# Batch norm streamed through one NeuronCore: stores moved from SyncE's DMA queue to ScalarE's

## The chip, the core and the metric

The kernel runs on one NeuronCore of one Trainium2 chip. The metric is the device time of one execution in microseconds (us), lower is better. A data transfer is issued by the sequencer of an engine (SyncE, written SP in the profile, or ScalarE, written ACT) and carried out by the core's 16 DMA engines. A *ring* is the list of work that one queue has waiting at the DMA engines.

All timed runs told here were at clock 1.000.

## The reference

Batch normalisation with given statistics, in fp32: per channel a scale and a shift, nothing more.

```python
# x: (32, 256, 128, 128) float32; gamma, beta, running_mean, running_var: (256,)
def reference(x, gamma, beta, running_mean, running_var):     # cut: reshapes to (1, 256, 1, 1)
    return gamma * (x - mean) / np.sqrt(var + 1e-5) + beta
```

x has 536.9 MB and so has the result. Every byte must be loaded once and stored once.

## The kernel before

A tile is 128 channels of one image: 128 partitions x 16384 floats, 8.39 MB. There are 64 tiles and three buffers. Parameters are turned into one scale and one shift per channel at the start; then VectorE does one multiply-add per tile in place.

```python
SINGLE_QUEUE = True
NBUF = 3
...
    def issue_load(i):
        if i >= NT:
            return
        t = data.tile([P, HW], mybir.dt.float32, tag="t")
        loads[i] = nc.sync.dma_start(out=t[:], in_=xr[i])
        tiles[i] = t

    for i in range(NBUF):
        issue_load(i)
    # ... (parameters, scale_t, shift_t: cut)

    def compute(i):
        t = tiles[i]
        cb = i % NCB
        nc.vector.tensor_scalar(out=t[:], in0=t[:],
            scalar1=scale_t[:, cb : cb + 1], scalar2=shift_t[:, cb : cb + 1],
            op0=mybir.AluOpType.mult, op1=mybir.AluOpType.add)

    def store(i):
        t = tiles.pop(i)
        (nc.sync if SINGLE_QUEUE else nc.scalar).dma_start(out=outr[i], in_=t[:])

    K = NBUF - 1
    for b in range((NT + K - 1) // K):
        idxs = [i for i in range(K * b, K * b + K) if i < NT]
        for i in idxs: compute(i)
        for i in idxs: store(i)
        for i in idxs: issue_load(i + NBUF)
```

Load i+3 waits for store i, because it writes into the same buffer. All transfers leave on SyncE's queue, in the order two stores, two loads. (The framework that compiles this orders instructions itself; the compiled order was read back.)

## Time and profile before

| | before |
|---|---|
| median of the first 3 runs | 2487.14 us (2486.58 to 2490.18) |
| span of the profiled run | 2488.1 us |
| VectorE busy | 564.7 us, 23% |
| DMA busy, of 16 engines | 99.8% of the span on queue q1 |
| bytes moved, mean rate | 1073.77 MB, 432 GB/s |

The page of the kernel before, parts 1 to 3. In the rows of 40 slices each digit is the busy share in tenths (9 is 90% or more), and GB/s is what the DMA engines moved in that slice.

```profile
span 2488.1 us, 378 instructions
DVE 564.7 (23%) x69; ACT 1.6 (0%) x2; POOL 3.2 (0%) x8
...
DMA  9999999999999999999999999999999999999998
GB/s 414 429 438 433 433 429 437 436 430 431 435 436 433 428 437 436 434 428 436 433 437 428 435 435 435 426 437 436 435 427 435 436 438 426 434 437 436 432 431 378
...
q1 hardware_dynamic: 18432, 1073.75, 99.8%
```

The DMA row has no slice under 9 but the last. A nine can hide up to a tenth of idle time, so this row alone does not show that there is no hole (k1_forced, below, has forty nines and loses 8%). The share of 99.8% on q1 does, and so do the records of the single packets: from the first data packet of the kernel to the last, an engine is idle for 4.0 us in the mean. There is hardly a hole for a change of queues to fill.

The list of waits of the kernel before: engine and line, what it waited for, total us, times, longest. First the engines' own list, then that of the SyncE queue.

```profile
DVE t L86 <- DMA t<-in_x_dram: 1867.9, 63, 49.6
```

```profile
SPq L48 <- DMA out_dram<-t: 1484.0, 61, 30.2
SPq L97 <- DVE t L86: 919.2, 33, 46.4
```

SyncE spends nearly the whole span waiting, 1484 us of it in loads that need a store to finish. But a wait of the issuing sequencer costs time only if the rings run empty meanwhile. The timeline of the kernel before shows why they don't (start, duration, engine, line; "x2" is two issues merged, and the duration then reaches from the first to the last):

```profile
1014.93 19.65 SPq L48 DMA_DIRECT2D t<-in_x_dram  x2
1034.63 28.62 SPq L97 DMA_DIRECT2D out_dram<-t  x2
1054.07 8.81 DVE L86 TENSOR_SCALAR t<-t,scale_t,shift_t 128x16384 f32<-128x16384 f32 x1 [49.61 <-DMA t<-in_x_dram]
1072.99 8.81 DVE L86 TENSOR_SCALAR t<-t,scale_t,shift_t 128x16384 f32<-128x16384 f32 x1 [10.12 <-DMA t<-in_x_dram]
1092.30 19.59 SPq L48 DMA_DIRECT2D t<-in_x_dram  x2
```

Two loads go out about 19.3 us apart, each at the moment a store has landed. When the first of them is issued, the second store is still in the ring; when the second is issued, the first load is. VectorE needs 8.8 us for a tile while the second load takes 19.3. There is always a transfer behind the one that moves.

The records of the single DMA packets say the same more finely. There are 16384 data packets of 65536 bytes, 8 per engine and transfer. The median packet takes 2418 ns, for loads and stores alike, and a new group of 128 packets (one transfer) starts every 19.319 us. The records do not name the engine; where this text speaks of one engine, its packets were chained by matching each packet's start to the end of the one before.

### The profile page before, as it was taken

How to read it: one execution, taken by the hardware profiler on the slowest of the kernel's cores; microseconds unless marked ns; L12 is line 12 of the kernel's file. 1: busy time of each engine (PE TensorE's matmuls, PEld its weight loads, DVE VectorE, ACT ScalarE, POOL GpSimd, SP SyncE). 2: the span in 40 equal slices, each digit the busy share in tenths (PEclk: the TensorE clock that was granted, in tenths of full speed). 3: DMA queues.
4: the chain of work that ended last, by engine and by line, in shares of the span. 5: the costliest groups of instructions: out<-in, count | busy, mean ns of one | idle time of the engine just before them, and what ended most of it. 6: DMA issues, size and time to landing. Idle time of an engine off the chain costs nothing.

```text
span 2488.1 us, 378 instructions
## 1 busy us (share of the span) xinstructions
DVE 564.7 (23%) x69; ACT 1.6 (0%) x2; POOL 3.2 (0%) x8
## 2 busy tenths in 40 slices
DVE  2122211222112221122212222121221212212121
ACT  0000000000000000000000000000000000000000
POOL 0000000000000000000000000000000000000000
DMA  9999999999999999999999999999999999999998
GB/s 414 429 438 433 433 429 437 436 430 431 435 436 433 428 437 436 434 428 436 433 437 428 435 435 435 426 437 436 435 427 435 436 438 426 434 437 436 432 431 378
DMA packets 18562, 1073.77 MB, mean 432 GB/s; under 512 B 2176, under 2 KB 2176, under 8 KB 2176
## 3 DMA queue, kind: packets, MB, share of 16 engines
q1 hardware_dynamic: 18432, 1073.75, 99.8%
q0 software_dynamic: 128, 0.00, 0.0%
q14 instruction: 2, 0.02, 0.0%
HBM read 536.88 MB, written 536.87 MB: 432 GB/s over the span
## 4 chain that ended last, share of the span: by engine, by line
DMA 51%; another core or an unknown queue 36%; DVE 11%; SPq 0%; issue 0%; POOL 0%; DVEq 0%; POOLq 0%; PEldq 0%
DMA t<-in_x_dram 48%; DVE t L86 11%; DMA out_dram<-t 2%; DMA t<-in_running_mean_dram 1%; SPq L97 0%; POOL t L56 0%; DVEq L86 0%; POOLq L133 0%; SPq L48 0%; DVE shift_t L81 0%; DVE tmp_t L80 0%; DVEq L80 0%; PEldq L133 0%
## 5 line engine op out<-in xcount | busy, mean ns | idle before, releaser
L86 DVE TENSOR_SCALAR t<-t,scale_t,shift_t 128x16384 f32<-128x16384 f32 x64 | 564.0, 8812 | 1868.0 <-DMA t<-in_x_dram 1867.9
L78 DVE RECIPROCAL tmp_t<-tmp_t 128x2 f32<-128x2 f32 x1 | 0.2, 166 | 13.2 <-ACT tmp_t L71 13.2
L80 DVE TENSOR_TENSOR tmp_t<-t,scale_t 128x2 f32<-128x2 f32 x1 | 0.2, 160 | 7.6 <-DMA t<-in_running_mean_dram 7.6
L71 ACT ACT_TABLE_LOAD x1 | 1.3, 1283 | 12.4 <-DMA t<-in_running_var_dram 12.4
L79 DVE TENSOR_TENSOR scale_t<-t,tmp_t 128x2 f32<-128x2 f32 x1 | 0.2, 160 | 3.2 <-DMA t<-in_gamma_dram 3.2
L56 POOL DMA_DIRECT2D t<-in_running_var_dram x1 | 0.8, 839 | 0.8 <-PEq L133 0.8
L56 POOL DMA_DIRECT2D t<-in_gamma_dram x1 | 0.7, 722 | 0.0
L56 POOL DMA_DIRECT2D t<-in_beta_dram x1 | 0.7, 722 | 0.0
L56 POOL DMA_DIRECT2D t<-in_running_mean_dram x1 | 0.7, 722 | 0.0
L71 ACT ACTIVATE tmp_t<-t,eps_t 128x2 f32<-128x2 f32 x1 | 0.3, 295 | 0.0
L65 DVE MEMSET eps_t<- 128x1 f32 x1 | 0.1, 59 | 0.8 <-PEq L122 0.8
L81 DVE TENSOR_TENSOR shift_t<-t,tmp_t 128x2 f32<-128x2 f32 x1 | 0.2, 160 | 0.0
L122 POOL MEMSET const-bfloat16-1.0<- 128x1 bf16 x1 | 0.1, 96 | 0.0
L122 POOL MEMSET const-uint8-127<- 128x1 uint8 x1 | 0.1, 94 | 0.0
L122 POOL MEMSET const-float32-0.0<- 128x1 f32 x1 | 0.1, 93 | 0.2 <-issue 0.2
L122 POOL MEMSET const-float32-1.0<- 128x1 f32 x1 | 0.1, 93 | 0.0
## 6 DMA issues: line engine op xcount, KB each, us to landing
t<-in_x_dram SPq DMA_DIRECT2D x64, 38.6
out_dram<-t SPq DMA_DIRECT2D x64, 49.9
t<-in_running_var_dram POOLq DMA_DIRECT2D x1, 1.0 KB, 11.1
t<-in_gamma_dram POOLq DMA_DIRECT2D x1, 1.0 KB, 15.2
t<-in_beta_dram POOLq DMA_DIRECT2D x1, 1.0 KB, 19.5
t<-in_running_mean_dram POOLq DMA_DIRECT2D x1, 1.0 KB, 21.6
```

The costliest lines, as they stand in the source:

```text
L56: nc.gpsimd.dma_start(out=t, in_=ap_1d.rearrange("(j p) -> p j", p=P))
L65: nc.vector.memset(eps_t, eps)
L71: nc.scalar.activation(out=tmp_t[:], in_=var_t[:], func=mybir.ActivationFunctionType.Sqrt, bias=eps_t[:], scale=1.0,)
L78: nc.vector.reciprocal(out=tmp_t[:], in_=tmp_t[:])
L79: nc.vector.tensor_mul(out=scale_t[:], in0=gamma_t[:], in1=tmp_t[:])
L80: nc.vector.tensor_mul(out=tmp_t[:], in0=mean_t[:], in1=scale_t[:])
L81: nc.vector.tensor_sub(out=shift_t[:], in0=beta_t[:], in1=tmp_t[:])
L86: nc.vector.tensor_scalar(out=t[:], in0=t[:], scalar1=scale_t[:, cb : cb + 1], scalar2=shift_t[:, cb : cb + 1], op0=mybir.AluOpType.mult, ...
L122: nc = _bacc.Bacc("TRN2", target_bir_lowering=False, num_devices=1)
```

## The change

The intent: loads on SyncE's queue and stores on ScalarE's, so that both rings hold work for the DMA engines at once and a load that waits for a buffer cannot hold up a store behind it. The Trainium skill, "Perfetto Trace Analysis", section "DMA Optimizations", suggests such a split: one issuing engine for inputs and another for outputs, "Especially when there are loops or control-flow", to "allow more dynamic spread".

```diff
-SINGLE_QUEUE = True
+SINGLE_QUEUE = False
 NBUF = 3
```

## The prediction

> What bounds the kernel now: the 16 DMA engines. The utilisation slices show DMA at 9 tenths or more in all slices but the last and 414 to 438 GB/s; the mean is 432 GB/s and queue q1 took 99.8% of 16 engines' span. VectorE is busy 564 us (23%) in 64 operations of 8.8 us; the list of waits has it waiting 1868 us for loads. In the DMA packet records each of the 16384 data packets (64 KB) takes 2418 ns, load or store alike, and packets follow each other on an engine without a gap: a whole 8 MB transfer starts every 19.319 us, and this step is the same after a change of direction. An estimate from that: 128 transfers x 19.319 = 2472.8 us of engine time, against a span of 2488.1. Only about 15 us (0.6%) are not pure transfer: some 2.5 us before the first packet, a slow first transfer (21.2 us), a few steps of 19.4 to 20.0 us, and 6 to 8 us of uneven engine finish at the end.
>
> 64 KB in 2418 ns is 27.1 GB/s an engine. The Trainium skill, "DMA: Bandwidth & Descriptors", section "Where 436 GB/s comes from", puts the ceiling at 435.2 GB/s for 16 engines; the trace agrees, with 432 to 438.
>
> What the change does: it adds and removes no work. The 64 stores go from SyncE's queue to ScalarE's, which is otherwise idle (1.6 us). Issuing costs about 0.34 us per transfer, already hidden. SyncE's waits (1484 us of loads for stores, 919 us of stores for VectorE) split over two queues, but they are off the critical path: while SyncE waits, the ring still holds a transfer, so no engine starves. The change removes waits that cost nothing.
>
> What moves: instead of load, load, store, store in one ring at full speed, a load and a store share the engines, so each should take about twice 19.3 us. The skill (same page, "Issuing engines are not separate DMA queues") says such transfers interleave on the same engines and only issue time is saved. With three buffers I expect no hole: an estimate by hand with 38.6 us per shared transfer and 12 us from load landed to store issued (8.8 of VectorE, about 3 of landing and issue) leaves 8 to 15 us of slack on either ring in the steady state; when one ring is empty the other runs at full speed.
>
> On the critical path, then, only the rate of a packet counts. If alternating rings costs nothing, the time is 2480 to 2490. If each switch costs some ns (the gap at a change of transfer is 2 to 3 ns, against -4 inside one), 16384 switches over 16 engines add about 6 us. If reads and writes mixed all the time are slower than in blocks, it costs more; the trace hardly shows that mix, only about 2 us per boundary in which the engines' skew overlaps both, without a slower packet.
>
> Predicted: 2492 us, 8 in 10 within 2478 to 2525. Faster by over 2%: 0.03; within 2%: 0.82; slower by over 2%: 0.15.
>
> What would show it: two hardware queues with half of the packets each; loads and stores near 40 us or more from issue to landing; still 430 to 436 GB/s in every slice; VectorE's waits for loads still about 1870 us, evenly near 30 us each instead of 49 and 10.
>
> What would make it wrong. Faster: if an engine can overlap a load's and a store's data, the rate would pass 440 GB/s. Slower: packets longer than 2418 ns without more in flight, so GB/s below 424 in steady slices; or holes in the DMA slices, because arbitration favours one ring so much that three buffers run dry.

## The result, and the profile after

| | before | after |
|---|---|---|
| median of the first 4 runs | 2487.09 us | 2494.76 us |
| lowest, highest | 2486.58, 2490.18 | 2487.87, 2500.81 |
| span of the profiled run | 2488.1 us | 2486.1 us |
| ratio after / before | | 1.0027, 95% interval 1.0007 to 1.0047 |

A ratio is the mean time of one kernel's fast runs over that of the other's of the same rounds, so it is not quite the ratio of the medians. Note the four single times of the changed kernel: 2487.87, 2500.81, 2499.87, 2489.64. They come in two groups, and the median falls between them.

The page of the changed kernel:

```profile
span 2486.1 us, 439 instructions
DVE 564.7 (23%) x69; ACT 1.6 (0%) x2; POOL 3.2 (0%) x8
...
DMA  9999999999999999999999999999999999999999
GB/s 414 429 438 435 429 435 433 439 428 434 437 438 428 434 437 439 428 432 438 431 428 438 434 428 433 433 433 429 432 431 435 432 430 431 429 439 430 430 435 405
...
q1 hardware_dynamic: 9216, 536.88, 50.1%
q10 hardware_dynamic: 9216, 536.88, 49.8%
```

There are now two hardware queues, q1 with the loads and q10 with the stores, each with half of the packets. The rate is 428 to 439 GB/s in all slices but the first and the last, where the kernel before had 426 to 438. The waits of the changed kernel, the engines' first, then the SyncE queue's:

```profile
DVE t L86 <- DMA t<-in_x_dram: 1873.5, 63, 30.8
```

```profile
SPq L48 <- DMA out_dram<-t: 2377.4, 61, 75.0
```

VectorE waits just as long as before (1873.5 against 1867.9 us), but evenly: at most 30.8 us, where it was 49 and 10 by turns. SyncE now waits 2377 us for stores, more than before, and nothing comes of it. The timeline, cut to one period (three short stretches of it):

```profile
1005.96 0.33 SPq L48 DMA_DIRECT2D t<-in_x_dram  x1
```

```profile
1018.19 8.81 DVE L86 TENSOR_SCALAR t<-t,scale_t,shift_t 128x16384 f32<-128x16384 f32 x1 [29.74 <-DMA t<-in_x_dram]
1027.03 0.34 ACTq L97 DMA_DIRECT2D out_dram<-t  x1
```

```profile
1044.62 0.33 SPq L48 DMA_DIRECT2D t<-in_x_dram  x1
```

A load is issued at 1005.96, about 12 us before the load ahead of it has landed and released VectorE at 1018.19. A store is issued at 1027.03, 17.6 us before the store ahead of it has landed and released the next load at 1044.62. So each ring has its next transfer 12 to 17 us before it needs it. The period, 1044.62 - 1005.96 = 38.66 us for a load and a store, is twice the 19.319 us of one transfer: the same work rate in another order.

The issue-to-landing medians of the page after (part 6) rose, 38.6 to 51.1 us for a load and 49.9 to 56.1 for a store, because each transfer now gets half of the engines' time:

```profile
t<-in_x_dram SPq DMA_DIRECT2D x64, 51.1
out_dram<-t ACTq DMA_DIRECT2D x64, 56.1
```

### The profile page after: what moved, and what is told of

It is laid out like the page before. It is cut to its first block, busy times and chain, and to the rows that moved or that the text cites. A ratio compares the mean times of both kernels' runs of the same rounds, so it can differ in the third digit from the quotient of the medians.

```text
span 2486.1 us, 439 instructions
## 1 busy us (share of the span) xinstructions
DVE 564.7 (23%) x69; ACT 1.6 (0%) x2; POOL 3.2 (0%) x8
## 3 DMA queue, kind: packets, MB, share of 16 engines
q1 hardware_dynamic: 9216, 536.88, 50.1%
q10 hardware_dynamic: 9216, 536.88, 49.8%
## 4 chain that ended last, share of the span: by engine, by line
another core or an unknown queue 75%; DVE 23%; DMA 1%; issue 0%; DVEq 0%; POOL 0%; POOLq 0%; PEldq 0%
DVE t L86 23%; DMA t<-in_running_mean_dram 1%; DVEq L86 0%; POOL t L56 0%; POOLq L133 0%; DVE shift_t L81 0%; DVE tmp_t L80 0%; DVEq L80 0%; PEldq L133 0%
## 5 line engine op out<-in xcount | busy, mean ns | idle before, releaser
L86 DVE TENSOR_SCALAR t<-t,scale_t,shift_t 128x16384 f32<-128x16384 f32 x64 | 564.0, 8813 | 1873.5 <-DMA t<-in_x_dram 1873.5
## 6 DMA issues: line engine op xcount, KB each, us to landing
t<-in_x_dram SPq DMA_DIRECT2D x64, 51.1
out_dram<-t ACTq DMA_DIRECT2D x64, 56.1
t<-in_beta_dram POOLq DMA_DIRECT2D x1, 1.0 KB, 19.3
```

Source lines behind the costliest of these rows:

```text
L86: nc.vector.tensor_scalar(out=t[:], in0=t[:], scalar1=scale_t[:, cb : cb + 1], scalar2=shift_t[:, cb : cb + 1], op0=mybir.AluOpType.mult, ...
```

## The experiments

The first theory: a DMA engine has one data path of about 27.1 GB/s (65536 bytes in 2418 ns) for both directions, it was already full, and what two queues could give, the kernel before already had from its order of two stores and two loads. Rivals: loads and stores have separate ceilings that two rings could use at once; the rings' order and number don't matter at all; and, for the two groups of times, an idle stretch at the end, slower packets, or single slow engines.

### loads_only and stores_only: is there a second data path?

```diff
 # loads_only: all loads and computes, only the last tile is stored (wrong result on purpose)
-            store(i)
+            if i == NT - 1:
+                store(i)
+            else:
+                tiles.pop(i)
```

> Wrong result on purpose: all 64 loads and computes, only the last tile is stored. One data path per engine (mine): a load packet takes 2418 ns as in the full kernel, so 65 transfers x 19.32 us = 1256 us, plus about 15 of start, last compute and tail: 1262 to 1280 us. Rival, a load and a store can overlap inside an engine and each direction alone has its own ceiling: then this run would also take about 1256, but together with stores_only the sum of the two would be clearly above the time of the changed kernel (2488 to 2500). Mine: the two sums, less what each runs of the other direction, equal it within 1%.

```diff
 # stores_only: three loads and computes, then 64 stores out of those buffers (wrong on purpose)
     def issue_load(i):
-        if i >= NT:
+        if i >= NBUF:
+            tiles[i] = tiles[i % NBUF]
             return
 # ... compute(i) returns for i >= NBUF; store(i) reads tiles[i] without popping it
```

> Wrong result on purpose: 3 loads and computes, then 64 stores out of those three buffers. Mine: 67 transfers x 19.32 = 1294 us plus about 10 to 20 of start and tail: 1300 to 1315 us, packets of 2418 ns. Rival (directions have separate ceilings, or stores alone are faster than mixed): packets shorter than 2400 ns or a rate above 440 GB/s.

Measured: 1277.51 and 1303.77 us, both in the expected ranges. The busy time of the stretch from 300 to 1200 us, whose last two columns are the DMA share and the GB/s, first of loads_only, then of stores_only, then of the kernel before, then of the changed kernel:

```profile
300.00:1200.00 900.00, 410.95 (x47) 0.00 (x0) 0.00 (x0) 1.00 1.00 433
```

```profile
300.00:1200.00 900.00, 0.00 (x0) 0.00 (x0) 0.00 (x0) 1.00 1.00 433
```

```profile
300.00:1200.00 900.00, 199.31 (x23) 0.00 (x0) 0.00 (x0) 1.00 1.00 434
```

```profile
300.00:1200.00 900.00, 202.70 (x23) 0.00 (x0) 0.00 (x0) 1.00 1.00 434
```

Loads alone, stores alone and both at once on two rings all run at 433 to 434 GB/s. The sum 1277.5 + 1303.8 less the three loads and one store that were extra (4 x 19.32) is 2504.0 us, 0.6% above the changed kernel's median over 12 runs (2488.8), and each of the two runs has a start and an end of its own. There is no second path for the other direction. The first theory stands on this point. One rival is left: that the limit is not in each engine but in something that all 16 share, such as the memory. A later trace speaks against it: in after_r5 only two of the 16 engines are at work from 2465.5 to 2475 us, and each of their packets takes 2418 ns there too.

### k1_single: a test that tested nothing

```diff
-    K = NBUF - 1
+    K = 1
```

> The kernel before with batches of one instead of two: store, load, store, load on the one queue. Mine: the change was worth nothing because the batching already kept a transfer in the one ring; without it each load waits for the only transfer in the ring, so the ring runs dry once per tile, for 1.5 us (landing 0.5, issue to first packet 1.0) up to 3 us (plus the engines' uneven finish of about 1.4): 61 x 1.5 to 3 = 92 to 183 us, so 2580 to 2670 us, 4 to 7% slower. On two queues the same program is instruction for instruction the changed kernel (the streams of each engine are the same), so that is what two queues would then be worth. Rival: the ring's order doesn't matter and the engines find work anyway: within 1% of before.

Measured: 2490.52 us, ratio 1.0007 (0.9992 to 1.0021). That contradicts the expectation, and the reason is trivial: the compiled instructions of this kernel are the same as those of the kernel before, in the same order (the numbers in the buffers' names differ). The scheduler paired two stores and two loads by itself. The run is one more run of the kernel before and says nothing for or against either theory.

### k1_forced: what an unpaired order costs on one queue

```diff
-        loads[i] = nc.sync.dma_start(out=t[:], in_=xr[i])
+        with after_last():      # tc.issue_after(the DMA issued last): an issue order, no wait
+            loads[i] = nc.sync.dma_start(out=t[:], in_=xr[i])
+        last[:] = [loads[i].ins]
 # ... the same around the store
-    K = NBUF - 1
+    K = 1
```

> The run k1_single tested nothing: its compiled instructions are those of the kernel before, in the same order (the scheduler pairs two stores and two loads by itself). Here the order store, load, store, load is forced on the one queue (checked in the compiled order). Mine: each load then waits for the only transfer in the ring, the ring runs dry once per tile, for 1.5 us (landing 0.5, issue to first packet 1.0) up to 3 us (with the engines' uneven finish): 61 x 1.5 to 3, so 2580 to 2670 us, and since two queues with the same order per stream are the changed kernel, that much is what two queues are worth against an unpaired order. Rival: order doesn't matter, the engines find work anyway: within 1% of before.

Measured: 2719.15 us (2718.87 to 2719.97), ratio 1.0924 (1.0908 to 1.094). The result is correct and the direction is as expected; the size was above my range. The same stretch of this kernel, three rows of its page, and its timeline:

```profile
300.00:1200.00 900.00, 185.06 (x21) 0.00 (x0) 0.00 (x0) 1.00 0.95 394
```

```profile
DMA  9999999999999999999999999999999999999999
GB/s 417 386 401 398 389 399 388 401 387 386 400 401 401 386 386 401 386 401 401 386 399 388 401 386 401 386 400 401 387 401 386 386 401 401 400 378 394 401 396 406
...
q1 hardware_dynamic: 18432, 1073.75, 95.5%
```

```profile
999.68 8.81 DVE L95 TENSOR_SCALAR t<-t,scale_t,shift_t 128x16384 f32<-128x16384 f32 x1 [33.70 <-DMA t<-in_x_dram]
1018.99 0.33 SPq L56 DMA_DIRECT2D t<-in_x_dram  x1
1019.37 0.42 SPq L107 DMA_DIRECT2D out_dram<-t  x1
1042.33 8.81 DVE L95 TENSOR_SCALAR t<-t,scale_t,shift_t 128x16384 f32<-128x16384 f32 x1 [33.84 <-DMA t<-in_x_dram]
1061.59 0.33 SPq L56 DMA_DIRECT2D t<-in_x_dram  x1
1061.96 0.43 SPq L107 DMA_DIRECT2D out_dram<-t  x1
```

The DMA row is full of nines, and only the GB/s row and the 95.5% give the loss away. The store's tile was ready at 1008.49, when VectorE ended it, but the store stood behind a load that waited for its buffer, and went out at 1019.37. So load and store now go out together, 0.4 us apart, once in 42.6 us instead of 38.6, and between two pairs there is nothing in the ring: 394 GB/s. In the packet records there are 61 moments with no data packet in flight on any engine, 1.33 us each in the median. A restart also costs more than the empty time: the first packet of each engine after it takes 3066 ns in the mean instead of 2418 (0.65 us more), and the eighth 3677 ns (1.26 us more). These make 3.2 us; the step from restart to restart is 42.53 us, 3.89 over 2 x 19.32. The rest, about 0.65 us, is what engines lose by ending and starting at different moments (an estimate, the remainder). I had counted the empty time and the uneven end, not the longer packets after it. From the first data packet of the run to the last, an engine is idle for 121 us in the mean (4 in the kernel before) and its packets take 113 us longer in sum: the loss is half empty time, half longer packets. Why the first and the eighth packet (the last one of the load) are long was not found.

With the stores on the other queue this program compiles to the changed kernel, every engine's instructions the same but for the numbers in the buffers' names. It was compiled and compared, and not run again. So against this order the change is worth 2719 to 2489 us, over 8%. Against the pairing order it is worth nothing.

### nbuf2_single and nbuf2_split: two buffers, one queue or two

```diff
-NBUF = 3
+NBUF = 2
 # nbuf2_split also has SINGLE_QUEUE = False
```

> Two buffers, one queue; the compiled order is again two stores, two loads. Mine: the second store covers the wait of the first load and the second load covers VectorE (19.3 us of load against about 10.5 from landing to issue), so the ring never runs dry: within 0.5% of before, 2480 to 2500 us. Rival (a third buffer is what keeps the engines full): over 2540 us.

> Two buffers, two queues. Mine: now the two buffers move as they come free, and twice in two tiles both rings are empty for about 1 us or more (one buffer in VectorE, the other between its store and its load): by hand 79.1 us for two tiles instead of 77.3, and the engines' drift on top: 2520 to 2600 us, slower than the same on one queue. Rival (two rings always fill the engines better): at most the time of nbuf2_single.

Measured: 2489.08 us (ratio 1.0003, 0.9988 to 1.0018) on one queue and 2667.6 us (1.0709, 1.0686 to 1.0733) on two. The stretch of nbuf2_single, then that of nbuf2_split:

```profile
300.00:1200.00 900.00, 202.68 (x23) 0.00 (x0) 0.00 (x0) 1.00 1.00 433
```

```profile
300.00:1200.00 900.00, 193.87 (x22) 0.00 (x0) 0.00 (x0) 1.00 0.98 402
```

With two buffers the change has the opposite sign: two rings are 7% slower than one. The compiled order on one queue is still two stores, two loads, as its timeline shows:

```profile
1043.05 20.14 SPq L97 DMA_DIRECT2D out_dram<-t  x2
```

```profile
1073.33 19.65 SPq L48 DMA_DIRECT2D t<-in_x_dram  x2
```

The second store covers the wait of the first load, and the second load covers VectorE. On two queues nothing holds the transfers in pairs, and again and again one buffer is in VectorE while the other has just been stored and not yet been reloaded: at 31 moments no data packet is in flight on any engine, 0.47 us each in the median. My estimate of the empty time was about right (1.8 us for two tiles by hand; in the packets the engines' mean idle time is 62.6 us over the 32 pairs, 2.0 each), and the range was missed by a term like that in k1_forced: busy time too went up, from 2481 us per engine in the kernel before to 2605, because a tenth of the load packets took 3293 ns or more (the first packet of a load took 3269 ns in the mean). These longer packets are two thirds of the loss, and their cause stays open. The rival "two rings always fill the engines better" is out, and so is "a third buffer is what keeps the engines full".

### after_r5: where do the times near 2500 come from?

> The changed kernel again, five rounds, for the spread of its times (2488, 2490, 2500, 2501 so far, where before has 2487 to 2490). If its spread comes from the engines' state in a run, both values come again, within one chip; if it was the one chip's, they don't. Either way the ratio to before lies between 1.000 and 1.006.

Edit: none, the changed kernel again. Measured: 2500.77, 2500.47, 2483.36, 2482.87, 2482.23, 2501.16 us; ratio 1.0011 (0.9983 to 1.0039). Both groups came on one chip, while the kernel before stayed between 2485.95 and 2493.58. This time the profiled run was a late one, of 2499.0 us. The ends of two runs of the same kernel, from 2400 to 2500 us in slices of 2.5 us: first the 2486.1 us run, then the 2499.0 us run.

```profile
DMA  9999999999999999999999999999999990000000
GB/s 419 419 419 419 419 419 472 524 419 446 419 419 446 419 419 419 419 419 419 419 419 419 419 419 419 446 419 419 446 419 472 419 446 0 0 0 0 0 0 0
```

```profile
DMA  9999999999999999999999941111119999999910
GB/s 419 419 419 419 419 446 446 419 472 419 419 419 446 446 419 419 498 472 419 472 446 446 419 184 79 79 52 52 52 52 419 419 419 419 419 419 419 419 52 0
```

From about 2460 to 2475 us nearly everything is idle, about 14 us as the engines' mean, and then the last store runs alone for 20 us. The timeline of that run has VectorE on the last tile from 2466.87 to 2475.7, and the store issued at 2475.71. It looked as if this idle stretch were the cause: the last load lands late, VectorE works, nobody has anything to move.

### after_tail4: quarter the last tile

```diff
 # the changed kernel, with the last tile loaded, computed and stored in four column quarters
-        loads[i] = nc.sync.dma_start(out=t[:], in_=xr[i])
+        for a, z in parts(i):       # one part, or four for the last tile
+            loads[i] = nc.sync.dma_start(out=t[:, a:z], in_=xr[i][:, a:z])
 # ... compute and store alike
```

> The changed kernel with the last tile loaded, computed and stored in four column quarters. The trace of the 2499 us run shows about 14 us in which nearly all engines stand idle at the end, while VectorE works on the last tile after a load that the engines finish 26 us apart; the 2486 us run has no such hole (load spread 3 us). Mine: the hole is the cause of the values near 2500, so quartering takes most of it (hole at most 5 us): all runs within 2480 to 2492 us. Rival (the drift of the engines itself or slower packets cost the time): values near 2500 come again in about half of the runs.

Measured: 2505.86, 2499.73, 2490.65, 2491.76, 2490.51, 2484.3 us. The ratio is 1.0019 (0.9996 to 1.0042). Late runs came again, so the expectation failed. The test was not clean either: the quarters' packets have 16 KB instead of 64, and in the profiled run (2504.1 us) VectorE got quarters up to 18.7 us apart, with about 15 us of idle time still there after 2440 us. It weakened the theory of the idle stretch without deciding.

### after_s62: work for every engine while VectorE does the last tile

```diff
-        (nc.sync if SINGLE_QUEUE else nc.scalar).dma_start(out=outr[i], in_=t[:])
+        (nc.sync if i == NT - 2 else nc.scalar).dma_start(out=outr[i], in_=t[:])
```

> The changed kernel, but the store of the last tile but one is issued on SyncE's queue behind the last load, so that while VectorE works on the last tile every engine has that store's data to move. Theory of the idle stretch at the end (my first, weakened by after_tail4): values near 2500 vanish, all runs within 2480 to 2492. Rival, now preferred: in the slow kind of run one or two engines are 15 to 25 us behind all others because their load packets were stretched more, they are never idle at the end (in the 2499 us trace two engines finish the last store but one at 2478.4 and go straight on to the last one), and the idle of the other 14 costs nothing: values of 2496 to 2506 come again in a good part of the runs.

Measured: 2499.41, 2481.19, 2482.72, 2500.88, 2482.9, 2482.49 us; ratio 0.9993 (0.997 to 1.0017). Late runs came again, two of six, though the last store but one now stood behind the last load. By itself this does not rule the idle stretch out, for in the profiled run, a late one (2497.7 us), most engines were idle again while VectorE did the last tile (2458.22 to 2467.03). What rules it out is which engines end last. The slices from 2400 to 2500 us:

```profile
DMA  9999999999999999999999911119999999211000
GB/s 419 446 419 419 524 603 446 446 419 419 419 419 419 419 419 419 419 419 419 419 419 419 419 79 52 79 52 419 446 419 419 419 551 603 105 52 52 26 0 0
```

One engine moves about 27 GB/s, so 52 GB/s is two engines. For 10 us (slices 24 to 27) and again at the very end two of sixteen engines still work, and the rest have finished what they were given. In after_r5's trace it is the same: 52 GB/s for 10 us. The data packets there show 14 engines ending the last store but one between 2459.4 and 2465.0 us and the other two at 2478.2 and 2478.5. Those two then ended the last store at 2497.5 and 2497.8, 19.3 us later: they were not idle. In both traces the packets of the two late engines follow each other from 2440 us to the end with gaps of -4 to 2 ns. The other 14 waited, and their idle time cost nothing. It was a consequence, not a cause, and the theory of the idle stretch is out.

### after_b and after_c: does the spread go with the time?

> The changed kernel, once more, for its trace. If the slowest engine sets the time: a run over 2495 us has a spread of over 15 us between the first and the last engine at the end of a load in the last quarter, a run under 2492 one of under 10 us (3 us at 2486, 26 us at 2499 so far).

> As after_b: over 2495 us goes with a spread of over 15 us at the loads' end in the last quarter, under 2492 us with under 10 us.

Measured: 2483.58 and 2483.99 us, both early. Together with the other traces (the spread is the median over the last quarter, by time, of the distance between the first and the last engine's semaphore write at the end of a load; the stretch is the time over 2418 ns that the packets of one chained engine add up to. In the late runs the chains mix engines; there it is an estimate: from the first packet to the end of the last, less 1024 packets of 2418 ns, with 3.2 us added because the records overlap, and taking the engine as never idle):

| run of the changed kernel, or after_s62 | span | spread | largest stretch of one engine |
|---|---|---|---|
| after_b | 2481.8 | 4.0 us | about 4 us |
| after_c | 2482.2 | 3.1 us | not worked out |
| first profile | 2486.1 | 3.1 us | about 9 us |
| after_s62 | 2497.7 | 22.8 to 26 us | 21 to 22 us (estimate) |
| after_r5 | 2499.0 | 26.3 us | 23 us (estimate) |

The expected rule held in both runs, but no late run fell among them; the late side of the rule rests on the three late traces had before (after_r5, after_s62 and after_tail4, whose spread is 23 us). So: a run is as long as its slowest engine. In an early run all engines lose about the same few us, in a late one two engines lose some 20 us more than the rest (seen in the traces of after_r5 and after_s62). The stretched packets are nearly all loads: in the first profile the load packets add up to 7.5 us per engine over 2418 ns each, the stores to 0.1 us. What picks the two engines, and why their loads stretch, stays open. The kernel before has a mild form of it: eight of its engines end at 2477.7 to 2477.8 us of the span and the others up to 2486.9.

Over all runs the kernel before had 37 runs with a median of 2488.1 and a mean of 2488.4 us (2485.3 to 2493.6). The changed kernel had 12 with a median of 2488.8 and a mean of 2491.4 us: seven between 2482.2 and 2489.6, five between 2499.9 and 2501.2. The middle is the same and the spread is wider on both sides: five of the twelve are also faster than the fastest run of the kernel before.

No version tried beats both clearly. 128 transfers x 19.319 us are 2472.8 us, and the earliest runs are at 2481 to 2482; what is left is the start, the end and a few us of stretched packets.

## Why the prediction was right or wrong

The prediction, 2492 us and "within 2%", was right: the median of the first four runs was 2494.76.

- *DMA engines bind, and the change adds and removes no work.* Right. loads_only, stores_only and both kernels run at 433 to 434 GB/s. The ceiling of 435.2 GB/s that the Trainium skill states in "DMA: Bandwidth & Descriptors", section "Where 436 GB/s comes from", agrees with that, and here it holds for the two directions together. The same section says that for transfers between HBM (the chip's main memory, where x lies) and SBUF (the core's own, where the tiles lie) a limit of about 358 GB/s binds instead; with one core at work these runs moved 433 to 434, so the measurement decides.
- *SyncE's waits are off the critical path, since the ring always holds a transfer.* Right, and shown by making it false: with the order forced so that the ring runs empty (k1_forced), the same waits cost 231 us.
- *With three buffers no hole; 8 to 15 us of slack on the rings.* Right that there is no hole. The slack was 12.2 us for loads, in the range, and 17.6 us for stores, above it.
- *Loads and stores near 40 us or more each; VectorE's waits about 1870 us, evenly near 30; half of the packets on each queue.* Right: 51.1 and 56.1 us, 1873.5 us with 30.8 at most, 9216 packets each.
- *Still 430 to 436 GB/s in every slice.* Not met as written: 428 to 439, with 414 in the first slice and 405 in the last. The kernel before had 426 to 438, with 414 and 378 at its ends, so the range was too narrow from the start and the rate did not change.
- *Each switch between rings costs some ns, about 6 us in all.* Wrong, and it is the term that put my figure above the old time. In the first profile's chains about 12600 of 14500 neighbouring pairs change the ring, and the median gap there is -4 ns (the records overlap a little), the same as inside a transfer before. No cost of switching can be seen.
- *Reads and writes of memory mixed all the time might be slower.* Not seen: 434 GB/s in the long stretch of both kernels.
- *"Only about 2 us per boundary in which the engines' skew overlaps both".* Too small: the first and last engine of a transfer are 1.4 us apart at the start of the kernel before but 9.8 us near its end.

So the verdict came for the right reason, while the nearness of 2492 to 2494.76 is luck. The median of all twelve runs is near 2489, with a second group near 2500, and that group comes from engines falling behind, which the prediction had not thought of as something the change would alter.

Where the hoped-for gain went: it had been taken already. The pairing of stores and loads on one queue does what the second ring was to do.

## What to carry to other kernels

Before splitting loads and stores over two queues, look at what the DMA engines move: at 432 GB/s and a share of 99.8% the sequencer's waits cost nothing here, however long they were. A DMA row full of nines is not enough: k1_forced and nbuf2_split have one too, at 395 and 402 GB/s in the mean. Two rings help where a transfer that waits holds up one that could run (8% here when the order was bad), and they hurt where the one queue's order was keeping few buffers in step (7% with two buffers). Compare the compiled order before reading a result, and take several runs: a profile shows one, and two kinds of run can hide behind a median.

## What the Trainium skill lacked or had wrong

- "DMA: Bandwidth & Descriptors", section "Issuing engines are not separate DMA queues", says issuing from several engines "will only save the time on the sequencer it takes to initiate the DMA". For the kernel as it stood that agrees (2488.1 against 2488.8 us). It does not say what is lost when a transfer that waits stands in front of one that is ready: k1_forced on one queue takes 2719 us, its two-queue form (the changed kernel) 2489. And it can go the other way: 2489 us on one queue and 2668 on two with two buffers.
- The same page gives fixed costs and first-byte latencies for one DMA, but nothing on packets that take longer after the rings have run empty. Here an empty ring cost 3.9 us a time (k1_forced): 1.33 us with nothing in flight, first packets of 3.07 us and eighth packets of 3.68 us instead of 2.42, and the uneven end.
- The same page, section "Latency and other measured facts", says that two DMA engines (7 and 15) are usually slower, and its best guess, called uncertain, ties this to descriptor rings of GpSimd's path. Here nearly all data went through the hardware queues, and two engines still fell some 20 us behind in late runs (spread 26 us at 2499.0 us, 3 us at 2486.1). The records here don't name the engines, so whether they are the ones that the page means is not known.
- "Perfetto Trace Analysis", section "DMA Optimizations", names loops and control flow as the case for one issuing engine for inputs and another for outputs. It does not name what decided here, the order on the one queue and the number of buffers: the split was worth nothing, 8% or minus 7% by these.
